# Recurrence gates of an RG-LRU as products over 64 rows, both gates of a block in the 128 output columns

## The chip, the cores and the metric

The kernel runs on one core of one Trainium2 chip. The metric is the device time in microseconds of one execution; the kernel before was run three times. The profile is of one execution, and its times are counted from the first to the last instruction (the span).

## The reference

One layer of a decoder trunk, 2048 tokens of width 1024, in float32. The normalised input goes through one projection into 3072 columns. Of these, 2048 feed four heads of a gated linear recurrence (HGRN2), and 1024 feed an RG-LRU of width 512. Both outputs, 512 wide each, go through one output projection back onto the residual stream; a SwiGLU feed-forward (2816 wide) and a final norm follow. The change is in the gates of the RG-LRU:

```python
xc = conv_b + sum(x_pad[:, tap:tap + S] * conv_w[tap] for tap in range(CONV_WIDTH))
xblk = xc.reshape(B, S, LRU_BLOCKS, LRU_BLOCK_DIM)            # 8 blocks of 64
r  = sigmoid(einsum('bsnd,nde->bsne', xblk, wa).reshape(B, S, W) + ba)
ig = sigmoid(einsum('bsnd,nde->bsne', xblk, wx).reshape(B, S, W) + bx)
log_a = -LRU_C * r * softplus(-a_param)
a = exp(log_a)
b_in = sqrt(-expm1(2.0 * log_a)) * (ig * xc)
h = scan of h_t = a_t * h_{t-1} + b_in_t
y = h * gelu(gate_b)
```

The weights `wa` and `wx` are block-diagonal: each of the 8 blocks is a 64 by 64 matrix that mixes only its own 64 features.

## The kernel before

The 2048 tokens are worked off in two halves of 1024, each in two chunks of 512 (`c`). Features lie on the partitions and tokens along the free dimension, so one tile is 128 features by 512 tokens, and a TensorE product of 128 by 128 weights with such a tile fills one PSUM bank. The RG-LRU's 512 features are four units (`u`) of 128, so a unit holds two of the 64-wide blocks.

Each float32 operand is split into two parts, a rounded one and its remainder (`xh` and `xl`, `gwh` and `gwl`), and each product is three TensorE instructions: high by high, low weight by high, high weight by low.

In each half the input projection runs in eight steps `s`, even for a head of HGRN2 and odd for a unit of the RG-LRU, and within each over both chunks. One step and chunk is two groups of 24 products, `pa` and `pb` (lines 234 to 236). What follows them is cut in parts that are queued in `pend`: `run_pending` (L969) takes one part from each entry between `pa` and `pb` of a later step. For HGRN2 these are `hg_mid` (transposes `pk`, scores `pc`, state updates `pu`) and `hg_post` (outputs `po`); for the RG-LRU it is `lru_post`. `lru_pre` computes the convolution `xc` and its two parts `xh`, `xl`.

`lru_post` (L407) makes both gates of a unit. The two blocks of the unit stand on the diagonal of a 128 by 128 weight matrix, the rest of it zeros, one such matrix for `wa` and one for `wx`. Three products give `pr` (lines 411 to 413), three more `pi`. A sigmoid on ScalarE (ACT) reads each of them from PSUM (lines 416 and 417), adding the bias, a column of the parameter tile `par`. Tanh, exp and square root follow on ACT, five element-wise operations and the scan on VectorE (DVE).

PSUM has eight banks, four under the tag `mm` for `pa` and `pb`, four under the tag `aux`, among which `pk`, `pc`, `pu`, `po`, `pr` and `pi` take turns. SBUF tiles too come from tags with a fixed number of slots: `raw` (3) for weights as loaded, `late` (5) for short-lived pages, `bt` (14) for large blocks.

The code is written in program order; a planner, which runs a model of the timeline when the kernel is built, then sets the order of the instructions on each engine and the slot of each tile. An instruction whose slot or input is not yet there in that model lets later ones go first. The order on each engine is fixed from then on, and each engine keeps it on the chip.

`parameters` (L112) loads the columns `par` and the gate weights `graw` (128 by 1024, 512 KB) on SP's queue, copies them to `gwh` on ACT (L118) and makes the remainder `gwl` on DVE (L119). `_layout` (L1109) arranges the arrays on the host.

Of the kernel before, what the change touches and what calls it, by code (L numbers as in the profile page):

```python
# [9 lines left out]
F32R = mybir.dt.float32r  # L10
AF = mybir.ActivationFunctionType
ALU = mybir.AluOpType

P = 128
SEQ = 2048
D = 1024
KT = D // P
HEADS = 4
NU = 4
# [4 lines left out]
CW = 512  # L24
# [4 lines left out]
NPAIR = NF // 2  # L29

C_LB0, C_LB1, C_CONVW, C_CONVB, C_BA, C_BX, C_A, C_NW, C_HN = 0, 4, 8, 24, 28, 32, 36, 40, 48
N_COLS = 49


@with_exitstack
def hybrid_layer(ctx: ExitStack, tc: tile.TileContext, x, x_t, norm_w, cols, w_in, gate_w, w_out, w_gu, w_down, out):
    nc = tc.nc
    const = ctx.enter_context(tc.tile_pool(name="const", bufs=1))
    sb = ctx.enter_context(tc.tile_pool(name="sb", bufs=1))
# [14 lines left out]
    def block(nm, dt=F32R):  # L54
        return sb.tile([P, 4, CW], dt, tag="bt", name=nm, bufs=14)
# [4 lines left out]
    def rawt(nm, shape=(P, D)):  # L60
        return sb.tile(list(shape), F32, tag="raw", name=nm, bufs=3)
# [7 lines left out]
    def aux(nm):  # L69
        return psp.tile([P, CW], F32, tag="aux", name=nm)  # L70
# [17 lines left out]
    for i in range(2):  # L88
        s = const.tile([P, TPC, P], F32, name=f"sct{i}")
# [18 lines left out]
    mhalf = tiny()  # L108
    nc.gpsimd.memset(mhalf, -0.5)
    par = const.tile([P, N_COLS], F32, name="par")  # L110

    def parameters():  # L112
        nc.sync.dma_start(out=par, in_=cols)
        graw = rawt("graw")
        nc.sync.dma_start(out=graw, in_=gate_w)
        gw = block("gw").rearrange("p (s a) w -> p s (a w)", s=2)
        gwh, gwl = gw[:, 0, :], gw[:, 1, :]
        nc.scalar.copy(out=gwh, in_=graw)  # L118
        nc.vector.tensor_tensor(out=gwl, in0=graw, in1=f(gwh), op=ALU.subtract)  # L119
# [285 lines left out]


    def lru_post(u, gl, xc, xh, xl, y, nm):  # L407
        pr, pi = aux("pr" + nm), aux("pi" + nm)
        for m, pg in enumerate((pr, pi)):
            gs = slice((m * NU + u) * P, (m * NU + u + 1) * P)  # L410
            nc.tensor.matmul(pg, lhsT=gwh[:, gs], rhs=xh, start=True, stop=False)
            nc.tensor.matmul(pg, lhsT=gwl[:, gs], rhs=xh, start=False, stop=False)
            nc.tensor.matmul(pg, lhsT=gwh[:, gs], rhs=xl, start=False, stop=True)
        r, ig, t = late("r" + nm), late("ig" + nm), late("t" + nm)
        us = slice(u, u + 1)
        nc.scalar.activation(out=r, in_=pr, func=AF.Sigmoid, bias=par[:, C_BA + u : C_BA + u + 1])
        nc.scalar.activation(out=ig, in_=pi, func=AF.Sigmoid, bias=par[:, C_BX + u : C_BX + u + 1])

        nc.scalar.activation(out=t, in_=r, func=AF.Tanh, scale=msp[:, us])
        nc.scalar.activation(out=r, in_=r, func=AF.Exp, scale=nmsp[:, us])  # L420
        v.tensor_tensor(out=ig, in0=ig, in1=xc, op=ALU.mult)
        v.tensor_tensor(out=xc, in0=r, in1=r, op=ALU.mult)
        v.scalar_tensor_tensor(out=t, in0=xc, scalar=1.0, in1=t, op0=ALU.add, op1=ALU.mult)
        nc.scalar.activation(out=t, in_=t, func=AF.Sqrt)
        v.tensor_tensor(out=ig, in0=ig, in1=t, op=ALU.mult)
        v.tensor_tensor_scan(out=t, data0=r, data1=ig, initial=hst[:, us], op0=ALU.mult, op1=ALU.add)
        nc.gpsimd.tensor_copy(out=hst[:, us], in_=t[:, CW - 1 : CW])
        v.tensor_tensor(out=y[:, u, :], in0=t, in1=gl, op=ALU.mult)
# [680 lines left out]
def _layout(i):  # L1109
    import numpy as np  # L1110

    a = {k: np.asarray(t) for k, t in i.items()}
    W = 512

    def by_rows(w):
        n = w.shape[1] // W
        w = w.reshape(4, 2, P, n, W).transpose(3, 0, 2, 1, 4)
        return w.reshape(n * 4, P, D)

    def by_cols(w):  # L1120
        n = w.shape[1] // P
        return w.reshape(KT, P, n, P).transpose(2, 1, 0, 3).reshape(n, P, D)

    w = a["w_in"][0]
    q, f_, v_, g_, lx, lg = (w[:, j * W : (j + 1) * W] for j in range(6))
    units = [by_rows(v_)]
    for j in range(4):
        s = slice(j * P, (j + 1) * P)
        units += [by_cols(t[:, s]) for t in (q, f_, lx, lg)]
    units.append(by_rows(g_))  # L1130

    def col(t):
        return t.reshape(-1, 4, P).transpose(2, 0, 1).reshape(P, -1)

    cols = [col(t) for t in (a["hg_lb"], a["conv_w"][0], a["conv_b"], a["lru_ba"], a["lru_bx"], a["lru_a"])]
    cols = np.concatenate(cols + [a["mix_norm_w"][0].reshape(KT, P).T, a["hg_norm_w"][0][:, None]], axis=1)
    gate_w = np.zeros((P, 2, NU, P), np.float32)
    for m, t in enumerate((a["lru_wa"][0], a["lru_wx"][0])):
        for b in range(8):
            o = (b % 2) * 64  # L1140
            gate_w[o : o + 64, m, b // 2, o : o + 64] = t[b]
    return {
        "x": a["x"][0],
        "x_t": a["x"][0].T,
        "norm_w": np.stack([a["mix_norm_w"][0], a["ffn_norm_w"][0], a["final_norm_w"]]),
        "cols": cols,
        "w_in": np.concatenate(units, axis=0),
        "gate_w": gate_w.reshape(P, D),
        "w_out": by_rows(a["w_out"][0]),
        "w_gu": by_cols(a["w_gate_up"][0]),  # L1150
        "w_down": a["w_down"][0].reshape(NF, P, D),
    }
# [19 lines left out]
```

## Time and profile before

| | |
|---|---|
| time of three runs | 2129.46, 2133.41, 2135.24 us (median 2133.41) |
| span of the profiled execution | 2131.1 us |
| TensorE products (PE) busy | 2101.2 us, 99% |
| TensorE weight loads (PEld) busy | 1735.7 us, 81% |
| DVE busy | 1493.1 us, 70% |
| ACT busy | 1010.2 us, 47% |
| data moved by DMA | 262.84 MB, mean 123 GB/s |

The page gives no device time of the profiled execution itself; its span stands for it, 2.3 us below the median of the runs. Times in the rows are microseconds from the start of the span. In a timeline row stand the start, the duration, the engine, the line, the operation, and `out<-in`; in brackets the idle time before it and what ended it. TensorE's products are pipelined, so their durations overlap, and the distance between starts tells what one costs. A pass over a plain float32 operand is two instructions.

The stage with the recurrences lies at about 64 to 305 us in the first half and up to 725 us in the second. The output projection follows, and the feed-forward takes the rest of the span.

### The profile page before, as it was taken

To read this page: it belongs to the slowest core of one execution; us is meant where nothing else is said; L and a number is where in the kernel's file an instruction comes from. 1 tells how busy PE (TensorE), PEld (TensorE's weight loads), DVE (VectorE), ACT (ScalarE), POOL (GpSimd) and SP (SyncE) were. 2 spreads that over 40 slices of the span, in tenths; PEclk is the share of its full clock that TensorE was granted. 3 is DMA by queue.
4 is the path that set the end of the run, shared out by engine and by line. 5 is a ranking of instruction groups with operands and counts; after the bars stand their busy time and mean duration, and the time that the engine had idled before them with its cause. 6 is when DMAs were issued, how large, how long until landed. Compare 5 with 4: busy or idle time off the path is not lost.

```text
span 2131.1 us, 26161 instructions
## 1 busy us (share of the span) xinstructions
PE 2101.2 (99%) x9704; PEld 1735.7 (81%) x9704; DVE 1493.1 (70%) x2415; ACT 1010.2 (47%) x1647; POOL 82.2 (4%) x130
## 2 busy tenths in 40 slices
PE   8999999999999999999999999999999999999998
PEld 6887888888878888788888888888888888888887
DVE  6577664645776566877667669878867667669787
ACT  5577764535777644533333334335433333334333
POOL 2000001100000000000000000000000000000000
PEclk9999999999999999999999999999999999999999
DMA  6111104852111058433323257346423223257424
GB/s 216 61 40 40 40 20 160 282 162 69 31 39 40 20 174 260 156 112 99 106 93 129 89 187 253 109 136 205 143 94 119 95 90 123 94 206 252 156 88 143
DMA packets 138420, 262.84 MB, mean 123 GB/s; under 512 B 11186, under 2 KB 27570, under 8 KB 138292
## 3 DMA queue, kind: packets, MB, share of 16 engines
q1 hardware_dynamic: 138292, 261.17, 36.5%
q8 instruction: 76, 1.25, 0.2%
q14 instruction: 52, 0.43, 0.1%
HBM read 197.95 MB, written 63.18 MB: 123 GB/s over the span
## 4 chain that ended last, share of the span: by engine, by line
PE 83%; ACT 6%; DVE 5%; DMA 3%; issue 2%; SPq 0%; POOL 0%; DVEq 0%; POOLq 0%; ACTq 0%
PE quad_e L614 11%; PE quad_g L614 11%; PE quad_a L614 11%; PE pda L885 10%; PE pdb L885 6%; PE quad_f L614 5%; PE poh L246 2%; PE poh L247 2%; PE poh L248 2%; PE pb L236 2%; PE pb L234 2%; PE pb L235 2%; PE pa L234 1%; PE pa L235 1%; PE pg L248 1%
## 5 line engine op out<-in xcount | busy, mean ns | idle before, releaser
L614 PE MATMUL quad_f<-act_f,wgu_f 128*128 128x512 f32 x528 | 127.4, 389 | 1.8 <-DVE h L1050 1.7
L614 PE MATMUL quad_a<-act_a,wgu_a 128*128 128x512 f32 x528 | 127.5, 389 | 0.0
L614 PE MATMUL quad_g<-act_d,wgu_d 128*128 128x512 f32 x528 | 127.0, 389 | 0.2 <-DVE u L498 0.2
L614 PE MATMUL quad_g<-act_g,wgu_g 128*128 128x512 f32 x528 | 127.1, 390 | 0.0
L614 PE MATMUL quad_a<-act_b,wgu_b 128*128 128x512 f32 x528 | 127.1, 389 | 0.0
L614 PE MATMUL quad_e<-act_e,wgu_e 128*128 128x512 f32 x528 | 127.0, 389 | 0.0
L614 PE MATMUL quad_e<-act_c,wgu_c 128*128 128x512 f32 x528 | 126.9, 389 | 0.0
L614 PEld LDWEIGHTS quad_f<-act_f,wgu_f 128*128 128x128 f32 x528 | 99.0, 188 | 23.1 <-ACT act_g L207 2.1
L498 DVE TENSOR_TENSOR u<-u,quad_g 128x512 f32<-128x512 f32 x88 | 60.5, 687 | 80.9 <-PE quad_g L614 80.9
L614 PEld LDWEIGHTS quad_g<-act_d,wgu_d 128*128 128x128 f32 x528 | 99.0, 188 | 21.1 <-DVE u L498 0.6
L614 PEld LDWEIGHTS quad_e<-act_c,wgu_c 128*128 128x128 f32 x528 | 99.1, 188 | 20.6
L614 PEld LDWEIGHTS quad_g<-act_g,wgu_g 128*128 128x128 f32 x528 | 99.0, 188 | 20.8 <-DVE wgu_g L208 0.3
L614 PEld LDWEIGHTS quad_e<-act_e,wgu_e 128*128 128x128 f32 x528 | 99.0, 188 | 20.6
L614 PEld LDWEIGHTS quad_a<-act_b,wgu_b 128*128 128x128 f32 x528 | 99.0, 188 | 20.5
L614 PEld LDWEIGHTS quad_a<-act_a,wgu_a 128*128 128x128 f32 x528 | 98.9, 188 | 20.6 <-ACT act_c L207 0.2
L234 PE MATMUL pa<-xn,whi_in 128*128 128x512 f32 x256 | 101.7, 397 | 0.0
L236 PE MATMUL pb<-xn,whi_in 128*128 128x512 f32 x256 | 101.0, 395 | 0.0
L235 PE MATMUL pb<-xn,wlo_in 128*128 128x512 f32 x256 | 101.0, 394 | 0.0
L234 PE MATMUL pb<-xn,whi_in 128*128 128x512 f32 x256 | 100.9, 394 | 0.0
L235 PE MATMUL pa<-xn,wlo_in 128*128 128x512 f32 x256 | 100.6, 393 | 0.0
L236 PE MATMUL pa<-xn,whi_in 128*128 128x512 f32 x256 | 100.5, 393 | 0.0
L248 PE MATMUL poh<-whi_o,mx 128*128 128x512 f32 x256 | 99.9, 391 | 0.0
(331 smaller groups left out, 4940.9 us busy)
## 6 DMA issues: line engine op xcount, KB each, us to landing
raw<-in_w_gu SPq DMA_DIRECT2D x88, 512.0 KB, 3.8
raw_in<-in_w_in SPq DMA_DIRECT2D x48, 512.0 KB, 3.5
ao_p<-as SPq DMA_DIRECT2D x76, 256.0 KB, 2.6
raw_o<-in_w_out SPq DMA_DIRECT2D x32, 512.0 KB, 4.4
x<-in_x SPq DMA_DIRECT2D x32, 256.0 KB, 5.8
xrh<-in_x SPq DMA_DIRECT2D x32, 256.0 KB, 3.9
h<-h SPq DMA_DIRECT2D x32, 256.0 KB, 3.5
hn<-hths SPq DMA_DIRECT2D x32, 256.0 KB, 3.3
```

The source lines that it names most:

```text
L234: nc.tensor.matmul(ps, lhsT=whi[:, ks], rhs=hi, start=(k == 0), stop=False)
L235: nc.tensor.matmul(ps, lhsT=wlo[:, ks], rhs=hi, start=False, stop=False)
L236: nc.tensor.matmul(ps, lhsT=whi[:, ks], rhs=lo, start=False, stop=(k == KT - 1))
L246: nc.tensor.matmul(ps, lhsT=hi, rhs=whi[:, ks], start=(k == 0), stop=False)
L247: nc.tensor.matmul(ps, lhsT=hi, rhs=wlo[:, ks], start=False, stop=False)
L248: nc.tensor.matmul(ps, lhsT=lo, rhs=whi[:, ks], start=False, stop=(k == KT - 1))
L498: (e or v).tensor_tensor(out=out, in0=a, in1=b, op=op)
L614: nc.tensor.matmul(ps, lhsT=w[:, s, ks], rhs=x, start=first and k + n == 0, stop=k == 3 and n == 2, skip_group_check=not first)
L885: nc.tensor.matmul(ps, lhsT=x, rhs=y, start=first and q + n == 0, stop=q == gr.n - 1 and n == 2, skip_group_check=not first)
```

## The change

The four 64 by 64 blocks of a unit (two of `wa`, two of `wx`) are no longer set into two 128 by 128 matrices with zeros. Instead the weights of a unit are one array of 128 rows by 128 columns without zeros: rows 0 to 63 hold the first block's `wa` and `wx` side by side, rows 64 to 127 the second block's `wx` and `wa`. A product now takes 64 rows of it and the same 64 rows of `xh` or `xl`. Rows 0 to 63 go to the bank `pa` (called `pga` in a timeline), rows 64 to 127 to `pb` (`pgb`); each holds the recurrence gate of its block in one half of the partitions and the input gate in the other. The instructions alternate between the two.

There are still six products per call, each with 512 columns. The two sigmoids over 128 partitions become four over 64, each reading the half of a bank that holds its gate. For the input gate the source and the destination lie in different halves, so a second copy of its bias, with the halves exchanged, is added to `par`.

The gate weights in DRAM shrink from 1024 to 512 columns. `graw` moves from a `raw` slot to a `late` slot; the split weights `wgate` keep a `bt` slot, now requested at the start of the program.

```diff
-N_COLS = 49
+C_BXS = 49
+N_COLS = 53
...
+    wgate = sb.tile([P, 2, CW], F32R, tag="bt", name="wgate", bufs=14)
...
-        graw = rawt("graw")
+        graw = late("graw")
         nc.sync.dma_start(out=graw, in_=gate_w)
-        gw = block("gw").rearrange("p (s a) w -> p s (a w)", s=2)
+        gw = wgate
...
-        pr, pi = aux("pr" + nm), aux("pi" + nm)
-        for m, pg in enumerate((pr, pi)):
-            gs = slice((m * NU + u) * P, (m * NU + u + 1) * P)
-            nc.tensor.matmul(pg, lhsT=gwh[:, gs], rhs=xh, start=True, stop=False)
-            nc.tensor.matmul(pg, lhsT=gwl[:, gs], rhs=xh, start=False, stop=False)
-            nc.tensor.matmul(pg, lhsT=gwh[:, gs], rhs=xl, start=False, stop=True)
+        HP = P // 2
+        lo_, hi_ = slice(0, HP), slice(HP, P)
+        pa, pb = aux("pga" + nm), aux("pgb" + nm)
+        gs = slice(u * P, (u + 1) * P)
+        for w, x, start, stop in ((gwh, xh, True, False), (gwl, xh, False, False), (gwh, xl, False, True)):
+            for ps, rows in ((pa, lo_), (pb, hi_)):
+                nc.tensor.matmul(ps, lhsT=w[rows, gs], rhs=x[rows, :], start=start, stop=stop)
...
-        nc.scalar.activation(out=r, in_=pr, func=AF.Sigmoid, bias=par[:, C_BA + u : C_BA + u + 1])
-        nc.scalar.activation(out=ig, in_=pi, func=AF.Sigmoid, bias=par[:, C_BX + u : C_BX + u + 1])
+        for dst, c0, rows, ps, src in (
+            (r, C_BA, lo_, pa, lo_),
+            (r, C_BA, hi_, pb, hi_),
+            (ig, C_BXS, lo_, pa, hi_),
+            (ig, C_BXS, hi_, pb, lo_),
+        ):
+            nc.scalar.activation(out=dst[rows], in_=ps[src], func=AF.Sigmoid, bias=par[src, c0 + u : c0 + u + 1])
...
-    gate_w = np.zeros((P, 2, NU, P), np.float32)
-    for m, t in enumerate((a["lru_wa"][0], a["lru_wx"][0])):
-        for b in range(8):
-            o = (b % 2) * 64
-            gate_w[o : o + 64, m, b // 2, o : o + 64] = t[b]
+    bx = col(a["lru_bx"])
+    cols = np.concatenate([cols, np.concatenate([bx[64:], bx[:64]], axis=0)], axis=1)
+    wa, wx = a["lru_wa"][0], a["lru_wx"][0]
+    gate_w = np.concatenate(
+        [np.concatenate([wa[0::2], wx[0::2]], axis=2), np.concatenate([wx[1::2], wa[1::2]], axis=2)], axis=1
+    ).transpose(1, 0, 2)
```

More of the change, by code (lines that the diff above doesn't have):

```diff
@@ L1147, in _layout @@
         "w_in": np.concatenate(units, axis=0),
-        "gate_w": gate_w.reshape(P, D),
+        "gate_w": gate_w.reshape(P, W),
         "w_out": by_rows(a["w_out"][0]),
```

## The prediction

> **What bounds the kernel now.** I read the shares of the engines first, then the recurrence stage in both halves by windows, then the list of what TensorE waited for.
>
> ```profile
> span 2131.1 us, 26161 instructions
> PE 2101.2 (99%) x9704; PEld 1735.7 (81%) x9704; DVE 1493.1 (70%) x2415; ACT 1010.2 (47%) x1647; POOL 82.2 (4%) x130
> ```
>
> TensorE is busy for 99% of the span; 30 us of 2131 are left over. The change touches only the stage that contains `lru_post`, so I cut that stage out, 220 us in each half (columns: busy time and count of PE, PEld, DVE, ACT, POOL; then clock and DMA).
>
> ```profile
> 85.00:305.00 220.00, 214.04 (x1125) 177.52 (x1125) 157.06 (x355) 158.39 (x262) 18.04 (x23) 0.99 0.11 37
> 505.00:725.00 220.00, 214.67 (x1123) 178.62 (x1122) 156.26 (x354) 157.94 (x262) 17.90 (x23) 0.98 0.11 37
> ```
>
> Here too TensorE is the bound (97%), but ACT is at 72%, far over its 47% of the whole span, and all of TensorE's missing time is lost to a few waits on VectorE in the HGRN2 chain:
>
> ```profile
> PE pk L329 <- DVE lg L315: 6.5, 3, 2.9
> PE pu L354 <- DVE kut L331: 3.8, 2, 1.9
> PE po L372 <- DVE sct L349: 0.9, 2, 0.5
> ```
>
> So time that TensorE gains or loses in the gate products reaches the end, and work added to ACT reaches it only through these few places.
>
> **The gate products as they stand.** There are 16 calls (4 units, 2 chunks, 2 halves), 6 products each:
>
> ```profile
> L411 PE MATMUL pr<-xh,gw x16: 395/437/484, 107.8 to 721.0; 128*128 128x512 f32 x16
> ```
>
> The durations overlap, so a product is priced by the distance of starts. In the call at 166.9 us:
>
> ```profile
> 167.25 0.40 PE L412 MATMUL pr<-xh,gw 128*128 128x512 f32 x1
> 167.49 0.40 PE L413 MATMUL pr<-xl,gw 128*128 128x512 f32 x1
> 167.72 0.39 PE L411 MATMUL pi<-xh,gw 128*128 128x512 f32 x1
> 167.95 0.40 PE L412 MATMUL pi<-xh,gw 128*128 128x512 f32 x1
> 168.19 0.40 PE L413 MATMUL pi<-xl,gw 128*128 128x512 f32 x1
> 168.42 0.39 PE L236 MATMUL pb<-xn,whi_in 128*128 128x512 f32 x1
> ```
>
> From 167.25 to 168.42 are five steps, 0.234 us each. 96 products are 22.5 us, 1.1% of the span. After the change the count is still 6 per call, with as many columns streamed. Nothing is removed; the gain must come from the two row halves running at the same time, which would at most halve it: 48 x 0.234 = 11.2 us.
>
> **Do two tiles run together, and what does the switch cost?** The trace has no product over 64 rows, but it has products into 64 output partitions, L337, in pairs. The nearest rows:
>
> ```profile
> 87.31 0.60 PE L329 MATMUL pk<-ident,lg 128*128 128x128 f32 x4
> 87.84 0.13 PEld L337 LDWEIGHTS pc<-W,nx 128*64 128x64 f32 x1 [0.17 <-issue]
> ...
> 88.33 0.27 PE L337 MATMUL pc<-W,nx 128*64 128x128 f32 x1
> 88.33 0.27 PE L337 MATMUL pc<-eb,nx 128*64 128x64 f32 x1
> 88.44 0.27 PE L337 MATMUL pc<-W,nx 128*64 128x128 f32 x1
> ...
> 88.55 0.38 PE L337 MATMUL pc<-W,nx 128*64 128x128 f32 x2
> 88.86 0.19 PEld L235 LDWEIGHTS pa<-xn,wlo_in 128*128 128x128 f32 x1 [0.17 <-issue]
> 88.97 0.19 PEld L236 LDWEIGHTS pa<-xn,whi_in 128*128 128x128 f32 x1
> 89.19 0.40 PE L236 MATMUL pa<-xn,whi_in 128*128 128x512 f32 x1
> ```
>
> Two things are to be seen. The `eb` product starts with the `W` product at 88.33, and the next `W` follows 0.11 us later, which is what a 128-column pass takes alone: the narrower product is free. I carry this over to row halves: a pair costs one product. And at both borders of the block the weight load sat idle for 0.17 us and then ran in the open, where elsewhere it is hidden under the product before. The price of going in and out: from 87.31 to the start of the first wide product after it (89.19 - 0.23 = 88.96) are 1.65 us, in which 4 transposes and 8 `W` passes of 0.11 us stream for 1.32 us; 0.33 us are the switch. The gate loads are 128 columns wide and not 64; two wide loads stand 0.10 us apart (88.86, 88.97), so I add half of that, 0.05: **0.38 us for each uninterrupted run** of 64-row products. Bounds: 0, if a row tile that keeps all 128 columns needs no switch, and twice, 0.76, if the loads of the two halves follow each other and each side stops longer. I take 0.38, since both borders in the trace show the stop.
>
> The Trainium skill, "TensorEngine Tiling (Array Packing)", Key Properties, says that changing the tiling mode, not merely the tile, drains TensorE. The 0.17 us at both borders agree for column tiles; for row tiles no run here shows it, and by the rule the switch belongs in the sum, by its absence it would be left out, which is the first rival.
>
> **How many runs, how many pairs.** This depends on the order that the planner writes for TensorE. I followed all 16 calls in the timeline. Four (first at 166.9, last at 599.2 us) are one run of six, as above. Six (first at 127.0, last at 721.0) are four products of `xh` and, after others, two of `xl`, which came later from VectorE:
>
> ```profile
> 127.71 0.40 PE L412 MATMUL pi<-xh,gw 128*128 128x512 f32 x1
> 127.94 0.39 PE L236 MATMUL pb<-xn,whi_in 128*128 128x512 f32 x1
> ...
> 128.41 0.39 PE L413 MATMUL pr<-xl,gw 128*128 128x512 f32 x1
> ```
>
> Four (first at 224.5, last at 701.6) have all of `pr`, then others, then all of `pi`:
>
> ```profile
> 225.04 0.40 PE L413 MATMUL pr<-xl,gw 128*128 128x512 f32 x1
> ...
> 225.51 0.38 PE L372 MATMUL po<-v,sct 128*128 128x128 f32 x2
> 225.64 0.48 PE L411 MATMUL pi<-xh,gw 128*128 128x512 f32 x1
> ```
>
> `pi` starts just behind the first use of `sct`, that is, when `pc` has been read out: the four `aux` banks are taken by `pk`, `pc`, `pu`, `po`, and the second gate gets its bank only from `pc`. After the change `pa` and `pb` need the same two banks, so all of `pa` would again go ahead of `pb` and nothing pairs. The last two (107.8 and 526.2) are mixed, two products of `pr`, then `po`, then the other four:
>
> ```profile
> 526.72 0.38 PE L372 MATMUL po<-v,sct 128*128 128x128 f32 x2
> 526.86 0.48 PE L413 MATMUL pr<-xl,gw 128*128 128x512 f32 x1
> ```
>
> Here I count one pair. If the order stays, the pairs are 4x3 + 6x3 + 4x0 + 2x1 = 32, worth 32 x 0.234 = -7.5 us. The runs are 4x1 + 6x2 + 4x2 + 2x2 = 28, costing 28 x 0.38 = +10.6 us. By kind: a run of six gains 0.32, four plus two lose 0.06, three plus three lose 0.76. **Sum on TensorE: +3.1 us.** Bounds: -7.5 with a free switch, +10.6 with no overlap.
>
> **The sigmoids.** Two of 128 partitions become four of 64.
>
> ```profile
> 114.67 0.69 ACT L416 ACTIVATE r<-pr,par 128x512 f32<-128x512 f32 x1
> 115.26 0.68 ACT L417 ACTIVATE ig<-pi,par 128x512 f32<-128x512 f32 x1
> L388 ACT COPY xp<-pa 128x512 f32<-128x512 f32 x8 | 4.7, 581 | 5.9 <-PE pa L236 5.8
> L351 ACT COPY sct<-pc 32x384 f32<-32x384 f32 x8 | 3.7, 466 | 6.7 <-DVE sct L349 6.7
> ```
>
> ACT's time goes by the columns: 32 partitions by 384 take 466 ns, 128 by 512 take 581, about in the ratio of what each streams plus a start. So a half sigmoid costs as much as a whole one, 0.59 us from start to start, and each call adds 2 x 0.59 = 1.18 us to ACT, 18.9 us in all, 9.4 per half (158 to 168 of 220 us). `pa` is now freed by the third sigmoid and `pb` by the fourth. Queued behind them on ACT are the tanh and exp of the same call and the next head's `sf`, `lg`, `eb`; VectorE's chain to `lg` waits for these, and TensorE for `lg`:
>
> ```profile
> 203.76 0.63 PE L329 MATMUL pk<-ident,lg 128*128 128x128 f32 x4 [2.87 <-DVE lg L315]
> 259.84 0.29 DVE L318 TENSOR_TENSOR lg<-lg,G 128x128 f32<-128x128 f32 x1
> 260.29 0.61 PE L329 MATMUL pk<-ident,lg 128*128 128x128 f32 x4
> ```
>
> At 203.8 TensorE already waits, and with two calls ahead of that chain up to 2.4 us could be added; at 260.3 the margin is 260.29 - (259.84 + 0.29) = 0.16 us, so one call would show as 1.0. Twice over, for two halves: at most 6.8 us. At least 0: ACT idles elsewhere in the stage (5.9 us ahead of `xp`), and the planner may put other products ahead of `pk`. I take 1.2, one call's delay seen once, since the runs that lose time on TensorE give the chain room.
>
> **Set-up and memory.** The gate weights halve to 256 KB, and their copy and subtraction too:
>
> ```profile
> L118 ACT CAST gw<-graw x1: 1052/1052/1052, 21.3 to 21.3; 128x1024 fp32r<-128x1024 f32 x1
> L119 DVE TENSOR_TENSOR gw<-graw,gw x1: 1221/1221/1221, 22.9 to 22.9; 128x1024 fp32r<-128x1024 f32 x1
> ```
>
> That saves about 0.5 and 0.6 us of engines at 21 to 24 us, and on SP's queue a `raw` slot for the input weights queued behind it; `graw` takes one of five `late` slots instead. No wait of TensorE in its list falls there, its V products cover it: 0, within -0.6 to +0.6 if the cover went. `wgate` takes one `bt` slot for the whole kernel as `gw` did: 0.
>
> **The rivals.** First, *the switch is free for row tiles*: -7.5 + 1.2 = -6.3, 2127; with all 48 pairs and no loss on ACT -11.2, 2122. For it: all 128 columns stay in use. Against: the two idle weight loads above. Second, *the halves do not overlap*: 28 switches and no pair, +10.6 + 1.2 = +11.8, 2145. For it: only column pairs are seen to overlap; two row halves would write two banks at once, 128 partitions each, which no row shows. The Trainium skill, "TensorE: Matmul & The Clock Gate", Part 3, has four row tiles of 32 run 3.07 times as fast, which lowers this chance; no run here shows it. Third, *ACT decides*: the four added sigmoids at the two tight `pk` of each half pass on in full, +3.1 + 6.8 = +9.9, 2143; it decides once the delay exceeds the 0.16 us of margin and the order stays. Fourth, *the planner writes the six together* in each call: 16 x (-0.32) = -5.1, +1.2: -3.9, 2129.5; against it the banks and the late `xl`.
>
> **How the numbers follow.** The sum is 3.1 + 1.2 = +4.3 us on the span of 2131.1. The median of three runs is 2133.4 (2129.5 to 2135.2), 2.3 above the span for what lies around it; I carry the difference over: **2138 us**. Chances: forecast 0.42 (2134 to 2142), free switch 0.18, no overlap 0.15, ACT 0.15, six together 0.10. About 0.3% (6.4 us) is what measuring this kernel can tell from no change, so the borders are 2127 and 2139.8. Faster: nearly two thirds of the first rival and a little of the fourth, 0.13. Slower: the second and third and a quarter of the forecast, 0.41. Same: 0.46. Range 2126 to 2148, which leaves the best end of the first rival and the worst of the second and third out.
>
> **What would show it.** In the new timeline: `pga` and `pgb` products starting in pairs within 0.02 us, the next pair 0.23 later (else the second rival); an idle weight load of about 0.17 us at both borders of each run (else the first); trios of `pga` alone where `pc` was late; four sigmoids 0.59 us apart; the waits of `pk` for `lg` grown by no more than a few us (else the third). The forecast falls if the order of the products changes much, since the number of runs carries the sign.

## The result, and the profile after

| | before | after |
|---|---|---|
| time, median | 2131.86 us (four runs, 2129.46 to 2135.24) | 2156.94 us (four runs, 2154.93 to 2158.18) |
| ratio, 95% interval | | 1.0116 (1.0104 to 1.0128) |
| span of the profiled execution | 2131.1 us | 2155.8 us |

The change makes the kernel 25 us slower, 1.2%. The prediction was 2138 with a range from 2126 to 2148.

The first rows of the page of the changed kernel:

```profile
span 2155.8 us, 26208 instructions
PE 2112.8 (98%) x9704; PEld 1731.7 (80%) x9704; DVE 1494.5 (69%) x2415; ACT 1028.6 (48%) x1673; POOL 84.5 (4%) x130
```

The two stretches with the recurrences, by windows of the changed kernel (columns as in the prediction):

```profile
85.00:305.00 220.00, 209.10 (x1087) 167.56 (x1086) 151.06 (x346) 155.35 (x261) 18.32 (x22) 0.99 0.11 37
505.00:725.00 220.00, 210.24 (x1081) 168.95 (x1079) 155.49 (x363) 156.47 (x256) 16.78 (x21) 0.98 0.11 37
```

And what TensorE waited for:

```profile
PE pk L331 <- DVE lg L317: 12.9, 4, 3.7
PE tp_o L224 <- DVE v L1010: 5.3, 2, 2.7
PE po L374 <- DVE sct L351: 5.0, 3, 1.9
```

In the same 220 us TensorE is busy for 209 and 210 us where it was 214 and 215, and it gets through 38 to 42 products fewer. (The second stretch holds somewhat earlier work than before, since the changed kernel is late by then.) The wait for `lg` has doubled, the one for `v` is new, and the one for `sct` has grown; the one for `kut` has shrunk, from 3.8 to 0.4 us. Against the kernel before, the first product of the output projection starts 11.7 us later in the first half and 23.4 us later in the second, and the end comes 24.7 us later: nearly the whole loss arises ahead of the two output projections, half in each half. A part of it lies behind the stretches above: the two waits for `v`, 2.65 us each, come at 325 and 756 us.

The clock has a part in it. The changed kernel shows five stretches of 3.4 us at half clock, as against three before. One of them, with the stall ahead of it, in the timeline and by windows (the clock is the third number from the end):

```profile
270.95 0.63 PE L331 MATMUL pk<-ident,lg 128*128 128x128 f32 x4 [3.62 <-DVE lg L317]
```

```profile
268.40:271.80 3.40, 0.85 (x11) 0.71 (x13) 3.40 (x8) 3.35 (x4) 1.13 (x1) 1.00 0.14 48
271.80:275.20 3.40, 3.40 (x20) 2.68 (x17) 3.40 (x12) 2.76 (x6) 0.00 (x0) 0.50 0.28 108
```

TensorE stands still for 3.62 us and then works for 3.4 us at half speed, so this stall costs some 1.7 us more than its own length. Not every stall does: no such stretch follows one of 2.80 us at 208.7 us in the same trace.

**The products.** The first pairs of the call at 184 us in the changed kernel:

```profile
184.22 0.39 PE L237 MATMUL pb<-xn,wlo_in 128*128 128x512 f32 x1
184.53 0.49 PE L416 MATMUL pga<-xh,wgate 64*128 64x512 f32 x1
184.54 0.49 PE L416 MATMUL pgb<-xh,wgate 64*128 64x512 f32 x1
184.87 0.39 PE L416 MATMUL pga<-xh,wgate 64*128 64x512 f32 x1
184.87 0.39 PE L416 MATMUL pgb<-xh,wgate 64*128 64x512 f32 x1
185.10 0.38 PE L416 MATMUL pga<-xl,wgate 64*128 64x512 f32 x1
185.11 0.38 PE L416 MATMUL pgb<-xl,wgate 64*128 64x512 f32 x1
185.42 0.50 PE L238 MATMUL pb<-xn,whi_in 128*128 128x512 f32 x1
185.76 0.39 PE L236 MATMUL pb<-xn,whi_in 128*128 128x512 f32 x1
```

and the weight loads at its two borders:

```profile
184.53 0.18 PEld L416 LDWEIGHTS pga<-xh,wgate 64*128 64x128 f32 x1 [0.35 <-issue]
185.42 0.19 PEld L238 LDWEIGHTS pb<-xn,whi_in 128*128 128x128 f32 x1 [0.36 <-issue]
```

The two halves of the rows do run together: both products of a pair start within 0.01 us, and the pairs stand 0.34 and 0.23 apart. From 184.22 to 185.76 are 1.54 us, in which the columns of one wide product, three pairs and another wide product streamed (five times 0.23); the remaining 0.39 us are the price of going in and out, and in the runs that stand between such wide products it came to 0.40 to 0.42. Where `pc` was late, the trios stand alone, as foreseen:

```profile
170.06 0.73 PE L416 MATMUL pga<-xh,wgate 64*128 64x512 f32 x2
170.64 0.39 PE L416 MATMUL pga<-xl,wgate 64*128 64x512 f32 x1
170.96 0.50 PE L236 MATMUL pb<-xn,whi_in 128*128 128x512 f32 x1
...
171.52 0.38 PE L374 MATMUL po<-v,sct 128*128 128x128 f32 x2
171.84 0.73 PE L416 MATMUL pgb<-xh,wgate 64*128 64x512 f32 x2
```

**The sigmoids.** ScalarE in the changed kernel:

```profile
250.81 0.69 ACT L425 ACTIVATE r<-pga,par 64x512 f32<-64x512 f32 x1
251.50 0.69 ACT L425 ACTIVATE ig<-pga,par 64x512 f32<-64x512 f32 x1
252.22 0.69 ACT L425 ACTIVATE r<-pgb,par 64x512 f32<-64x512 f32 x1
252.93 0.68 ACT L425 ACTIVATE ig<-pgb,par 64x512 f32<-64x512 f32 x1
253.64 0.60 ACT L257 ACTIVATE sf<-pb 128x512 f32<-128x512 f32 x1
```

Four of them take 2.83 us to the next instruction, 0.69 to 0.72 each. Before, `r` and `ig` stood 0.59 apart (114.67 and 115.26): the end of one overlapped with the start of the next. Now each starts only when the one ahead has ended.

### The profile page after: what moved, and what is told of

Same layout as the page of the kernel before. It is cut to its first block, busy times and chain, and to the rows that moved or that the text cites. A ratio compares the mean times of both kernels' runs of the same rounds, so it can differ in the third digit from the quotient of the medians.

```text
span 2155.8 us, 26208 instructions
## 1 busy us (share of the span) xinstructions
PE 2112.8 (98%) x9704; PEld 1731.7 (80%) x9704; DVE 1494.5 (69%) x2415; ACT 1028.6 (48%) x1673; POOL 84.5 (4%) x130
## 4 chain that ended last, share of the span: by engine, by line
PE 81%; ACT 8%; DVE 7%; DMA 2%; issue 2%; SPq 0%; DVEq 0%; POOLq 0%; POOL 0%; ACTq 0%
PE quad_e L622 11%; PE quad_g L622 11%; PE quad_a L622 11%; PE pda L893 10%; PE pdb L893 6%; PE quad_f L622 5%; PE poh L248 2%; PE poh L249 2%; PE poh L250 2%; PE pb L236 2%; PE pb L237 2%; PE pb L238 1%; PE pv L248 1%; PE pv L250 1%; PE pv L249 1%
## 5 line engine op out<-in xcount | busy, mean ns | idle before, releaser
L622 PEld LDWEIGHTS quad_a<-act_b,wgu_b 128*128 128x128 f32 x528 | 99.0, 188 | 20.5
L249 PE MATMUL poh<-wlo_o,mx 128*128 128x512 f32 x256 | 99.9, 393 | 0.6 <-DVE wlo_o L166 0.6
```

Source lines behind the costliest of these rows:

```text
L249: nc.tensor.matmul(ps, lhsT=hi, rhs=wlo[:, ks], start=False, stop=False)
L622: nc.tensor.matmul(ps, lhsT=w[:, s, ks], rhs=x, start=first and k + n == 0, stop=k == 3 and n == 2, skip_group_check=not first)
```

## The experiments

The theory at this point: the products cost a few us, as predicted, and the rest is ScalarE, whose half sigmoids delay the HGRN2 chain behind them. The rivals were the products, the planner's new order, and the set-up.

### The sigmoids alone and the products alone

Here `e1` has the products of before and halves the sigmoids; `e2` has the new products and two whole sigmoids. In both the planner writes its own order.

```diff
# e1, on the kernel before
-        nc.scalar.activation(out=r, in_=pr, func=AF.Sigmoid, bias=...)
-        nc.scalar.activation(out=ig, in_=pi, func=AF.Sigmoid, bias=...)
+        for dst, c0, ps in ((r, C_BA, pr), (ig, C_BX, pi)):
+            for rows in (slice(0, P // 2), slice(P // 2, P)):
+                nc.scalar.activation(out=dst[rows], in_=ps[rows], func=AF.Sigmoid, bias=...)
# e2, on the kernel after, in place of the four
+        nc.scalar.activation(out=r, in_=pa, func=AF.Sigmoid, bias=par[:, C_BA + u : C_BA + u + 1])
+        nc.scalar.activation(out=ig, in_=pb, func=AF.Sigmoid, bias=par[:, C_BX + u : C_BX + u + 1])
```

> The products of before (128 rows, no change of tile), but each of the two sigmoids cut into two over 64 partitions, as the change has them. ACT theory (the added ACT time, and the order that the planner then writes, delay the HGRN2 chain, and TensorE waits and drops to half clock): the waits grew by 12.7 us and the half-clock time by 3.3 us from before to after, so this kernel alone should be 12 to 17 us slower than before, about 2146, with waits of pk for lg of over 10 us. Switch theory (nearly all of the 25 us comes from TensorE changing its tile mode): within 3 us of before, 2130 to 2135.

> The 64-row products of the change, but two sigmoids over 128 partitions, one for each bank, as before. This leaves out that each gate gets its own half of a bank: r and ig hold both gates mixed, so the values are not the reference's; the amount of work is that of before. ACT theory: only the cost on TensorE is left, about 26 runs at 0.42 us less 30 pairs at 0.23, +4 us, so 2134 to 2139, with waits as before (about 18 us in all). Switch theory: 2150 to 2157.

The sigmoids alone took 2160.83 us beside 2132.48 (ratio 1.0126, 1.0111 to 1.0141), the products alone 2135.14 (1.0013, 1.0003 to 1.0022). TensorE's waits with the sigmoids alone,

```profile
PE tp_o L222 <- DVE v L1003: 11.7, 2, 5.9
PE pk L329 <- DVE lg L315: 10.6, 4, 3.0
PE po L372 <- DVE sct L349: 5.6, 6, 1.9
```

are those of the changed kernel in other shares. So the products cost 2.7 us (0.6 to 4.7 by the interval), where 3.1 was predicted, and the loss is in the sigmoids, or in the order that the planner writes once they are halved.

### The set-up, and the product of `xl`

```diff
# e4, on the kernel after: the slots of before
-        graw = late("graw")
+        graw = rawt("graw")[:, 0:CW]
-        gw = wgate
+        gw = block("gw")
# e5, on the kernel after: the product with xl first
-        for w, x, start, stop in ((gwh, xh, True, False), (gwl, xh, False, False), (gwh, xl, False, True)):
+        for w, x, start, stop in ((gwh, xl, True, False), (gwh, xh, False, False), (gwl, xh, False, True)):
```

> The changed kernel, but with the gate weights loaded into a raw slot and their split in a bt slot requested inside parameters, as before. If set-up and slots cost nothing, as the prediction had it: the time of the changed kernel, 2155 to 2159. If the moved slots cost something: at least 3 us less.

> The changed kernel with the product of xl first in each bank instead of last, so that the six products become ready together and a call whose xl is late is one run instead of two (six calls of 16). If the switches cost 0.4 us a run on the way that sets the end: 6 runs fewer and some pairs more, 2 to 4 us below the changed kernel, about 2153. If the waits behind ACT and the planner's order decide: they move by more than that, either way, with no fixed sign.

`e4` took 2157.98 us (1.0115, 1.0095 to 1.0135, from two runs), no other than the changed kernel within that interval: the set-up costs nothing that can be seen. `e5` took 2144.74 (1.0055, 1.0039 to 1.0072), 12 us less than the changed kernel. The list of runs does not explain it: it has 24 runs and 26 pairs in place of 26 and 30, which by the prices above is worth nothing. The planner wrote another order there, with 115 loads of function tables on ScalarE as against 109; the waits for `sct` are gone, and those for `v` are down to 1.1 us. Which part of that order was worth how much isn't separated.

### The order held

To take the planner out, the layer is built twice, the order of all five engines is read from the first build and written into the second as edges between neighbours; a gate's sigmoids count as one place.

```diff
# f1: four half sigmoids, products of before, in the order of the kernel before
# f3: the work of the kernel before, in the order of e1
# f2: the complete change, in the order of e2
+    order = _program(laid, ORDER_OF)[2]
+    nc, arrays, now = _program(laid, RUN, order)
# f5: as f2, but the six products of a call stand where the last of them stood
+            _hold(tc, traced, _together(traced, order))
```

> The 128-row products of before and four half sigmoids, but with every engine's order held to the order that the planner wrote for before (each sigmoid replaced by its two halves in place). In the runs so far a half sigmoid stands 0.70 us from the next one where a whole one stands 0.59, so a call adds 4 x 0.70 - 2 x 0.59 = 1.6 us to ACT, 26 us in all. Time theory (the longer ACT work itself delays the chain to lg and TensorE waits): 2148 to 2161, about as with the planner's own order. Order theory (the planner, told of the longer ACT work, writes another order, and that order does not suit the chip): 2133 to 2139.

> The products and the two whole sigmoids of before, so exactly its work, but every engine's order held to the one that the planner wrote for the kernel with four half sigmoids and 128-row products. Order theory: it keeps most of the loss, 2148 to 2158. Time theory: 2130 to 2138.

> The changed kernel, complete, with every engine's order held to the one that the planner writes for 64-row products with two sigmoids (the kernel that ran at 2135). Order theory: that kernel's time and a little for ACT, 2136 to 2143. Time theory: no better than the changed kernel, 2150 to 2160.

> As the run before in this call (the changed kernel in the held order), but the six gate products of each call are set together, in three pairs, at the place of the last of them: 16 runs instead of 26 and 48 pairs instead of about 30. By the prices read so far, 0.42 us for a run and 0.23 saved for a pair: 10 x 0.42 + 18 x 0.23 = 8 us below that run, 2128 to 2135 by the order theory. If a run of six costs more than that, or the products set back make ACT and VectorE late: no gain, or a loss.

Beside 2131.95: `f3` took 2132.28 (1.0002, 0.9992 to 1.0011), so the order that the planner wrote for the halves costs nothing with whole sigmoids, and as the cause it falls. (With the halves it is some 6.5 us dearer than the old one: `e1` lost 28.4, `f1` 21.9.) `f1` took 2153.82 (1.0108, 1.0092 to 1.0125): in the old order, with the old products, the half sigmoids alone cost 21.9 us. `f2` took 2157.25, as the changed kernel; the products, with the order that the planner wrote for them, add 3.4 to `f1`. `f5` took 2148.98, 8.3 less than `f2`. In the order of `e2` there are 28 runs and 32 pairs, so `f5` has 12 runs fewer, at 0.41, and 16 pairs more, at 0.23: 4.9 + 3.7 = 8.6.

The place where `f1` loses can be seen where the kernel before already waited. First its waits for `lg` in the list, then one of them in the timeline; that one was 2.87 us in the kernel before.

```profile
PE pk L329 <- DVE lg L315: 14.7, 7, 6.2
PE pk L329 <- DVE lg L318: 2.8, 2, 1.4
```

```profile
208.77 1.09 PE L329 MATMUL pk<-ident,lg 128*128 128x128 f32 x4 [6.18 <-DVE lg L315]
```

The 20 us around the end of this wait by windows, of the kernel before and then of `f1`, where the same work comes 5 us later:

```profile
185.00:205.00 20.00, 17.13 (x89) 13.92 (x88) 15.15 (x34) 19.73 (x25) 1.09 (x2) 1.00 0.08 27
```

```profile
190.00:210.00 20.00, 13.81 (x63) 11.03 (x63) 13.74 (x31) 19.71 (x24) 0.38 (x1) 0.87 0.08 27
```

ScalarE is busy for 19.7 of 20 us in both, and TensorE for 17.13 and 13.81. ScalarE is the bound here, and it was before the change, though its share of the whole span is 47%: in the kernel before it has no gap of more than 0.03 us between 171.6 and 206.7 us. Two gate calls lie in that stretch, and the wait at its end is longer by 6.18 - 2.87 = 3.31 us, which is what two calls add.

### Halves, or time

Is it the half partitions, the smaller writes into one tile, or plainly ScalarE's time? In the order of before, `g1` issues each whole sigmoid twice, and `g2` leaves most of the input gate out. `h1` has the products together, as in `f5`, and two whole sigmoids, as in `e2`: what the new products are worth if ScalarE has nothing added.

```diff
# g1
+            for rows in ((slice(0, P),) * 2 if FOUR[0] else (slice(0, P),)):
# g2: the input gate's sigmoid over 8 of 512 columns
+        for dst, c0, ps, n in ((r, C_BA, pr, CW), (ig, C_BX, pi, 8 if FOUR[0] else CW)):
+            m = nc.scalar.activation(out=dst[:, 0:n], in_=ps[:, 0:n], func=AF.Sigmoid, bias=...)
+        v.tensor_tensor(out=ig, in0=xc if FOUR[0] else ig, in1=xc, op=ALU.mult)
# h1, on f5
-ORDER_OF, RUN = False, True
+ORDER_OF, RUN = False, False
```

> The kernel before, in its own order, with each of the two whole sigmoids issued twice (the second writes the same values again). It adds 2 x 0.59 us a call to ACT, 18.9 us in all, with no half sigmoid. Four half sigmoids in this order added 16 x 1.63 = 26 us of ACT and cost 21.9 us of time, 0.84 us for each us. If the added ACT time is what costs: 18.9 x 0.84 = 16 us, about 2148. If it is something special to sigmoids over half the partitions: under 8 us, 2132 to 2140.

> The kernel before, in its own order, with the input gate's sigmoid over 8 columns instead of 512; the multiplication that reads it takes xc in its place. This leaves out the input gate, so the values are not the reference's. ACT has about 0.4 us a call less to do, some 6 us in all. If ACT time costs as much below the kernel before as above it (0.84): 5 us faster, 2127. If TensorE bounds as soon as ACT is not late: only a part of the waits goes, 0 to 2 us faster.

> 64-row products, the six of a call together in three pairs (16 runs, 48 pairs), with two whole sigmoids; as in the earlier kernel with two sigmoids the gates are mixed, so the values are not the reference's. It shows what the products over 64 rows are worth on TensorE without the added ACT time. The same step gave 8.3 us with four sigmoids: 2135 - 8.3 = 2127, about 5 us under the kernel before. If setting the products back makes the two gates late: 2132 or more.

Beside 2132.7: `g1` 2150.93 (1.0083, 1.0069 to 1.0097), `g2` 2128.91 (0.998, 0.997 to 0.999), `h1` 2129.07 (0.9984, 0.9975 to 0.9993). ScalarE in `g1` and in `g2`:

```profile
114.28 1.41 ACT L419 ACTIVATE r<-pr,par 128x512 f32<-128x512 f32 x2
115.58 1.40 ACT L419 ACTIVATE ig<-pi,par 128x512 f32<-128x512 f32 x2
116.89 0.71 ACT L422 ACTIVATE t<-r,tinies 128x512 f32<-128x512 f32 x1
```

```profile
115.53 0.69 ACT L417 ACTIVATE r<-pr,par 128x512 f32<-128x512 f32 x1
116.12 0.26 ACT L417 ACTIVATE ig<-pi,par 128x8 f32<-128x8 f32 x1
116.26 0.72 ACT L420 ACTIVATE t<-r,tinies 128x512 f32<-128x512 f32 x1
```

From `r` to `t` `g1` takes 2.61 us and `g2` 0.73, where the kernel before takes 1.16 and the half sigmoids take 2.82. So `g1` adds 1.45 x 16 = 23 us with no half tile in it and loses 18.2, and `g2` takes away 6.9 us and gains 3.8. It is ScalarE's time, not the halves as such. And the new products are worth 3.6 us if ScalarE is left as it was; the prediction's fourth rival had 5.1 for that, and 3.9 with 1.2 us of ScalarE.

### Work taken away from ScalarE

If ScalarE's time is what costs, taking some away anywhere in the stage should pay. The first try moved the rounding of `xc` to `xh`, 16 casts, to GpSimd, in the kernel before.

```diff
# k1
-        split((xh, xl), xc)
+        nc.gpsimd.tensor_copy(out=xh, in_=xc)
+        v.tensor_tensor(out=xl, in0=xc, in1=f(xh), op=ALU.subtract)
```

> The kernel before with one piece of ACT work of the recurrence moved to GpSimd: the rounded copy xh of xc (0.62 us a call on ACT, 16 calls, 9.9 us). Adding ACT time cost about 0.8 us for each us, and taking some 6 us away gained 3.8. If that holds for work moved away: 0.6 x 9.9 = 6 us faster than before, about 2126. If GpSimd is slower at it and xl on VectorE and the gate products wait for it, or the two engines get in each other's way: no gain, 2132 or more.

It took 2140.7 us beside 2133.63 (1.0042, 1.0028 to 1.0056), 7 us slower: a miss. Its page, its groups and its waits show why it does not test the theory:

```profile
PE 2101.9 (98%) x9704; PEld 1735.8 (81%) x9704; DVE 1496.3 (70%) x2415; ACT 1010.1 (47%) x1639; POOL 91.9 (4%) x146
```

```profile
L403 POOL CAST xh<-xc x16: 613/843/1540, 101.9 to 728.2; 128x512 fp32r<-128x512 f32 x16
```

```profile
PE pu L354 <- DVE kut L331: 14.3, 6, 3.0
```

ScalarE has 16 casts fewer and still the same 1010.1 us, with 1639 instructions, only 8 fewer than the 1647 of before. The planner's new order had brought eight more loads of function tables, 123 in place of 115, and the cast itself takes 0.84 us on GpSimd where ScalarE takes 0.62. How the 7 us divide between these isn't separated.

That pointed to the tables. A function of ScalarE needs its table loaded, and the kernel before changes them 115 times. One of its largest groups of loads, the group at the exp of `lru_post`, and one stretch of its ScalarE:

```profile
L254 ACT ACT_TABLE_LOAD x16 | 20.5, 1283 | 0.3
L420 ACT ACT_TABLE_LOAD x12 | 15.4, 1283 | 0.2
```

```profile
197.56 0.63 ACT L280 ACTIVATE lg<-lg 128x512 f32<-128x512 f32 x1
198.22 1.28 ACT L254 ACT_TABLE_LOAD   x1
199.51 0.60 ACT L254 ACTIVATE sq<-pa 128x512 f32<-128x512 f32 x1
```

115 x 1.283 = 148 us of ScalarE's 1010 are loads. After exp (`lg`, L280) a sigmoid (`sq`) needs one; a tanh after an exp needs none, as the rows of `m1` below show. It matters which table stands: the tanh of `lru_post` runs behind the sigmoids without a load in 14 of its 16 calls, and the exp that follows it in the program (L420) has one in 12. The next four runs write each sigmoid of the stage as 0.5 + 0.5 tanh(x/2) and fold the factors into what is there; the same values are computed, up to rounding. `m1` does it in the kernel before with its order held, `m2` with the planner's own order, `m4` in the complete change (as `f2`), `m5` with the products together (as `f5`).

```diff
# m1, m2, m4, m5
-        nc.scalar.activation(out=sq, in_=psq, func=AF.Sigmoid)
-        nc.scalar.activation(out=sf, in_=psf, func=AF.Sigmoid)
-        v.tensor_tensor(out=sq, in0=sq, in1=psq, op=ALU.mult)
-        nc.scalar.activation(out=lg, in_=sf, func=AF.Ln, scale=omlb[:, hs], bias=lb[:, hs])
+        nc.scalar.activation(out=sq, in_=psq, func=AF.Tanh, scale=0.5)
+        nc.scalar.activation(out=sf, in_=psf, func=AF.Tanh, scale=0.5)
+        v.scalar_tensor_tensor(out=sq, in0=sq, scalar=1.0, in1=psq, op0=ALU.add, op1=ALU.mult)
+        nc.scalar.activation(out=lg, in_=sf, func=AF.Ln, scale=halves["homlb"][:, hs], bias=halves["hlb"][:, hs])
...
-        func=AF.Sigmoid, bias=par[rows, c0 + u : c0 + u + 1]
+        func=AF.Tanh, scale=0.5, bias=b[rows, u : u + 1]
...
-        nc.scalar.activation(out=t, in_=r, func=AF.Tanh, scale=msp[:, us])
-        nc.scalar.activation(out=r, in_=r, func=AF.Exp, scale=nmsp[:, us])
-        v.tensor_tensor(out=ig, in0=ig, in1=xc, op=ALU.mult)
+        nc.scalar.activation(out=t, in_=r, func=AF.Tanh, scale=hm, bias=hm)
+        nc.scalar.activation(out=r, in_=r, func=AF.Exp, scale=hn, bias=hn)
+        v.scalar_tensor_tensor(out=ig, in0=ig, scalar=1.0, in1=xc, op0=ALU.add, op1=ALU.mult)
```

> The kernel before, its order of instructions held on all engines. Every sigmoid of the recurrence stage (two per gate call, two per head call) is written as 0.5 + 0.5 tanh(x/2), the factors folded into scales, biases and products that are there already: the same instructions, with another function. Tanh and exp stand under one function table in the traces, the sigmoid and exp do not, so 30 of ScalarE's 115 table loads of 1.283 us fall away, 38.5 us of ScalarE, spread over the stage and none of them a gate's sigmoid itself. Theory A, ScalarE's time in the whole stage decides: the columns left out in the earlier run gained 0.55 us per us of ScalarE, and the waits of TensorE on the chain behind ScalarE add up to some 11 us before, so faster by 6 to 12 us, 2121 to 2127. Theory B, only the time between the gate products and the release of their banks counts, which keeps its length here: within 2 us of before.

> The same as the run with the held order, but the planner writes the order anew: 87 table loads in place of 115, 36 us of ScalarE. Theory A: faster by 6 to 12 us, 2121 to 2127, as with the held order, since an order alone moved nothing in an earlier run. Theory B: within 2 us of before, or what a new order gives by itself.

> The complete change with the order of the version with two sigmoids held, which took 2157, and all sigmoids written by tanh: the four half gates stay four instructions of 0.70 us, and 30 table loads (38.5 us of ScalarE) fall away elsewhere. ScalarE then has some 12 us less to do than before the change. Theory A: the loss of 22 us that the four halves brought is gone, what is left is the 2.7 us of the products and a gain of some us, 2126 to 2136. Theory B, the four instructions at their place hold the banks and the chain of the gate: the loss stays, 2150 to 2157.

> As before it, but the six products of each call stand together in three pairs, which took 2149 with sigmoids. Theory A: 8 us below the run with the same four halves and scattered products, 2118 to 2129, so faster than the kernel before. Theory B: 2142 to 2149.

Beside 2133.05: `m1` 2114.49 us (0.9915, 0.9902 to 0.9929), `m2` 2114.47 (the same ratio), `m4` 2128.48 (0.998, 0.9971 to 0.9989), `m5` 2119.91 (0.994, 0.9926 to 0.9953). The times are those of theory A, that ScalarE's time in the whole stage counts: 28.8 us less from `f2` to `m4`, by work taken from ScalarE. But the two theories are less cleanly separated than was expected. Of the 30 loads that fall away, 10 stood between a call's products and its first sigmoid, so the banks are released sooner too. From the start of the last gate product to the end of the last gate sigmoid it takes, in the mean of the 16 calls, 5.5 us in the kernel before, 7.3 in `f1`, 7.6 in `f2`, 4.3 in `m1` and 6.2 in `m4`. Against theory B, that only this time counts, speaks that `m4` holds its banks longer than the kernel before and is 4.6 us faster; how much the release of the banks adds isn't separated.

`m1` gained more than the 6 to 12 us that were expected; it and `m2` are the fastest kernels here that compute the reference, 18.6 us below the kernel before. The page of `m1`, its windows, and the ScalarE rows that answer to those above:

```profile
PE 2095.2 (99%) x9704; PEld 1734.0 (82%) x9704; DVE 1493.0 (71%) x2423; ACT 972.4 (46%) x1617; POOL 85.1 (4%) x130
```

```profile
85.00:305.00 220.00, 220.00 (x1164) 183.92 (x1163) 160.83 (x362) 151.11 (x258) 18.31 (x23) 1.00 0.12 38
505.00:725.00 220.00, 220.00 (x1153) 184.06 (x1152) 160.49 (x346) 147.82 (x255) 19.88 (x23) 1.00 0.10 34
```

```profile
193.16 0.63 ACT L302 ACTIVATE lg<-lg 128x512 f32<-128x512 f32 x1
193.70 0.58 ACT L268 ACTIVATE sq<-pa 128x512 f32<-128x512 f32 x1
```

The load between `lg` and `sq` is gone. TensorE is busy for 220.00 of 220 us in both stages, its clock is 1.00, and the waits for `lg` and `kut` stand no longer in its list. The waits of the HGRN2 chain listed before (6.5, 3.8 and 0.9) and what TensorE lost in three stretches at half clock (half of the time that it worked in them, 4.9 us together) make 16 of the 18.6 us.

### What is left between the two versions

```diff
# n1: m1 with each gate in two halves
-ORDER_OF, RUN = False, False
+ORDER_OF, RUN = False, True
# n2: m5 with two whole gates
-ORDER_OF, RUN = False, True
+ORDER_OF, RUN = False, False
```

> The products and the held order of before, all sigmoids by tanh, and each gate's one instruction over 128 partitions split into two over 64: the 26.5 us that cost 21.9 us with 115 table loads, now with 85. In the version with two whole gates TensorE stands at 220.00 busy us of 220 in the recurrence stage and no longer waits for lg, so there is slack ahead of ScalarE's chain. Theory A (a saturated chain makes ScalarE's time cost): well under half of it reaches the end now, 3 to 10 us over the 2114.5 of two whole gates, 2117 to 2124. Theory B (the time at this place): again about 20 us, 2134.

> The products of the change, the six of a call together in three pairs, all sigmoids by tanh, and two whole gate instructions, one per bank, so that both gates lie mixed over the halves of the partitions and the values are not the reference's. Nothing is added to ScalarE. With TensorE the only bound, 16 calls save what the pairs save less one switch each, 0.70 - 0.40 = 0.30 us (0.32 by the prediction): 5 us under the 2114.5 of the products of before, 2109 to 2111. If the switch cost more, or the waits took the gain, 2113 to 2117.

`n2` took 2109.55 us beside 2133.93, 4.9 below `m1`, as expected (5.8 if each is set against the kernel before of its own call). With TensorE the only bound, 16 calls of six products together save 0.31 to 0.36 us each, where the prediction's fourth rival had 0.32. Its windows show TensorE at 220.00 again, in the first half:

```profile
85.00:305.00 220.00, 220.00 (x1180) 180.82 (x1179) 162.94 (x364) 152.00 (x262) 19.03 (x24) 1.00 0.12 37
```

`n1` took 2127.83, 13.3 more than `m1` (12.5 by the same reckoning), between the 3 to 10 of theory A and the 20 of theory B:

```profile
PE pk L351 <- DVE lg L337: 4.5, 6, 1.3
```

Even with 30 table loads gone, half of the 26 us that the half gates add reaches the end. Six waits of `pk` for `lg`, at most 1.3 us long, are back. Here too the banks are held longer than in the kernel before, some 6 us in the mean, and the kernel is 6.1 us faster.

ScalarE's busy time by the page, and the time against the kernel before of the same call, in kernels with the products and the order of before:

| kernel | ScalarE busy, us | less or more than before | time, less or more than before |
|---|---|---|---|
| `m1` | 972.4 | -37.8 | -18.6 |
| `n1` | 998.4 | -11.8 | -6.1 |
| `g2` | 1003.4 | -6.8 | -3.8 |
| before | 1010.2 | 0 | 0 |
| `g1` | 1030.7 | +20.5 | +18.2 |
| `f1` | 1034.6 | +24.4 | +21.9 |

Below the kernel before a us of ScalarE is worth about 0.5 us of time, above it about 0.9.

## Why the prediction was wrong

**The bound.** "Work added to ACT reaches it only through these few places" is the sentence that failed. The list of waits was right for the kernel before, but it names the places where the chain is late, not how much slack it has elsewhere. ScalarE was read as 72% busy over 220 us; in the 20 us up to 205 it is busy for 19.73. There every us added passes on. Idle time elsewhere does not help: just ahead of that stretch ScalarE waits 6.55 us for `pb`, and in `f1`, with the longer gates, still 6.54.

**The term for the sigmoids.** This is the step that made the error: of 18.9 us added to ScalarE, 1.2 was taken to reach the end, 6.8 at most. 21.9 did (`f1`). Two things were mis-sized. The smaller is the price: a half sigmoid stands 0.71 from the next instruction, not 0.59, so a call adds 2.82 - 1.16 = 1.66 us and not 1.18, 26.5 us in all. (The page shows only 18.4 us more, since the planner's order for the changed kernel also has 6 table loads fewer, 109 for 115: 26.5 - 7.7 = 18.8.) The larger is the bound. At the two places in each half that it counted, the delay came as it was reckoned, at the new price: in `f1` the first wait is 3.31 us longer, two calls, and at the second there is a wait of 1.45, about one call less the margin of 0.16. That makes 9.5 us for both halves, not 21.9. But the delay also comes at places that were not yet late: `f1` waits for `lg` at L315 seven times in place of three, and the changed kernel for `v` and `sct` too. Nor had the sum a term for the clock. In `f1` TensorE stands idle for 26.3 us between 60 and 800 us, where it was 11.8, and what it loses at half clock is 7.7 us in place of 4.9: together 17.4 of the 19.1 us between the spans of the two profiles. The rest isn't traced. With no slack shown in the stretches ahead of the waits, the bound should have been the time added, 26 us at a slope of one.

**The products.** The sum on TensorE was +3.1 us; measured +2.7 (`e2`) and +3.4 (`f2` against `f1`). Its parts hold as well: pairs overlap in full, a switch costs 0.40 to 0.42 where 0.38 was taken, and the 28 runs and 32 pairs that were counted are those of `e2` and `f2`; the changed kernel has 26 and 30. The weight load stood idle 0.35 us at either border, twice the 0.17 of the column tiles, and part of that lies under the stream. The Trainium skill, "TensorEngine Tiling (Array Packing)", Key Properties, has the mode change drain TensorE; the 0.35 us at both borders agree for row tiles too.

**The set-up** was put at nothing, and nothing is seen of it (`e4`).

**The rivals.** The free switch and the missing overlap fall by the rows above. The six together were put at 5.1 us on TensorE; without the half sigmoids they are worth 3.6 (`h1`) and 4.9 (`n2`), and with them `f5` is still 17 us slower than the kernel before. The third, "ACT decides", was the right mechanism: the delay passes the 0.16 us of margin, and `f1` loses with the order kept. Its price was 6.8 for what cost 22, so its time, 2143, was still 14 us off where the forecast was 19 off, and the range that was built on these prices ended at 2148.

**What would show it.** The text named "the waits of `pk` for `lg` grown by no more than a few us (else the third)": 6.5 to 12.9, the third. "Four sigmoids 0.59 us apart" came out as 0.71.

## What to carry to other kernels

An engine at 70% of a stage can be the bound in it: before work is added to an engine that feeds the bound, look at short windows that end where the bound waits, and without proof of slack price the addition at its full length. Splitting one ScalarE instruction over 128 partitions into two over 64 more than doubled its time here (0.58 to 1.41 us), so an arrangement that saves on TensorE has to leave whole tiles behind for the engine that reads them. And count what ScalarE spends on tables: writing the sigmoids by tanh, which needs no load behind an exp here, took 30 loads out and 18.6 us off this kernel, far more than the products could give.

## What the runs showed of the hardware

- Two sigmoids in a row overlap by 0.1 us when each covers 128 partitions and a tile of its own (0.59 apart, 0.69 long). A half of 64 partitions doesn't overlap with what follows, even if that writes another tile from another bank (252.93 to 253.64), nor do two whole ones that write the same tile (`g1`: 1.30 for two, 0.72 and 0.58). Why isn't settled.
- Most stalls of TensorE of some 2 to 6 us were followed in these traces by 3.4 us at half clock (after 2.87 us in the kernel before, after 3.62 and 2.65 in the changed one), but not all (not after 1.91 us at 268 us before, nor after 2.80 at 208.7 in the changed one). With the stalls gone (`m1`) the clock stayed at 1.00 throughout both stages.
- A change of function table took 1.28 us of ScalarE, and the next instruction started 0.01 us after it (198.22 to 199.51). The Trainium skill, "ScalarE: Activation LUTs", has tanh beside exp in one set (section "Table sets: the hidden batching unit"), with which `m1` agrees for a tanh behind an exp; its 2.66 us for a load with its drain (section "What ACT_TABLE_LOAD costs") is twice what these rows show.
- A cast of 128 by 512 took 0.61 to 1.54 us on GpSimd, 0.62 on ScalarE.
